# Sums of squares of q by products with a column of ones, and fewer transpositions of constants

## The chip, the core and the metric

The program runs on one core of a Trainium2 chip, in one launch. The metric is the device time in microseconds (us) of one execution. Three executions of the kernel before were timed: 1227.67, 1227.69 and 1228.21 us, median 1227.69 us. A fourth was profiled: 1226.6 us from its first to its last instruction.

The engines in the profile: PE (TensorE, the matrix engine; PEld are its loads of the stationary operand), DVE (VectorE), ACT (ScalarE), POOL (GpSimd) and SP (which here only issues transfers).

## What is computed

Two decoder layers with a residual stream of 512 positions by 1024 channels. The first has gated linear attention as its mixer, the second a gated DeltaNet; each is followed by a gated feed-forward network with a causal convolution of width 3, and each of the four sublayers ends in a layer norm. What concerns us is the second mixer, cut to its core:

```python
proj = x @ w_in
qkv, gate, beta_lin, a_lin = split(proj)
qkv = silu(causal_dwconv(qkv, conv_w))          # width 4
q, k, v = split(qkv)                            # 8 heads of 128 channels
qc = l2_normalize(q_by_head) * 128 ** -0.5      # x * rsqrt(sum(x*x) + 1e-6), per position and head
kc = l2_normalize(k_by_head)
m = tril(k_beta @ k.T * decay, -1)              # per head and chunk of positions
sol = triangular_solve(I + m, [v * beta, k_beta * exp(bcum)])
qk = q @ k.T * decay
# per chunk: v_new = u - w @ S ; o = q_dec @ S + qk @ v_new ; S = S * decay + k_dec.T @ v_new
y = (rms_norm(o, norm_w) * silu(gate)) @ w_out
```

The sum of squares of q, for each of 512 positions and 8 heads, is needed only at the very end: the kernel leaves q unscaled and folds 1/|q| into the scale of the output rows.

## The kernel before

All products are float32 or float32 split in two halves (`wh`, `wl` and `xh`, `xl`: three products stand for one). Activations lie with channels on the 128 partitions and positions along the row, except where a product needs it the other way round; then a 128x128 block is transposed on PE by a product with the identity (`tr`, line L226 of the profile, and `tr4` for four of them). All other products go through `mm` (L208).

The program is written as one main stream of large products (tiles `fm`, `tm`, `fold`) with small tasks between them. Tasks are Python generators; a planner's clock, `self.clk`, is moved on by an estimate for each product (0.11 us for a transposition, 0.00175 us per column for a float32 product), and after every few large products `pump` runs the tasks that are due. A task yields the time that it wants to wait. So the position of small work in the stream is set by these estimates. In the first stage the order on PE is fixed as written; from the second half of the first mixer on a scheduler may still move instructions of different tasks against each other. Each engine then runs its own list strictly in order.

The second mixer (`gdn`) first projects k (8 heads), then v, then q, one head for each `fm` bank of 24 large products. `gdn_conv` (L1541 to L1545) turns a bank into a head: one ACT operation, three on DVE, then SiLU on ACT. For each pair of q heads `q_done` starts `q_task` 6 planner microseconds later. `q_task` first calls `squares`: it transposes the four 128x128 blocks of each head into a PSUM bank `qT` (L226), so that positions lie on partitions, and eight ACT operations square a block each and sum its rows into `ssq` (L1625). Then it forms k-by-q products `pq` (L208) and DVE multiplies them into the decay matrix (L1682). `norms(0)` (L1818) turns `ssq` into 1/|q| once all eight heads are there.

Meanwhile `base` inverts 32x32 triangles for all heads and chunks at once, 31 pairs of DVE operations (L1703, L1705) spread over the projections. Its result `tt` is copied to `m` (L1708), both go to DRAM (`dinvt`, L1710; `dinv`, L1709), and come back laid out for PE, four pairs of heads one after another, in small transfers on the queues of SP and POOL: `T` (L1722) and `rm` (L1725). `inverses` then builds the 128x128 inverses from them in ten steps of small products with results `V` and `R`, each step at least 3.2 planner microseconds after the one before. Step 0 makes `V` of pair 0; step 1 makes `V` of pair 1 and, from the copied `V` of pair 0 (L1769 on ACT, L1770 on DVE), `R` of pair 0.

Rows of constants (layer norm weights, convolution taps) are loaded with channels along the row and transposed once by `columns`: one transposition and one copy for each set of rows, for the first mixer (sets of 4 and 2 rows) and, at planner time 64, for everything else (sets of 32, 32, 88, 44, 88, 44, 96 and 1 rows).

Of the kernel before, what the change touches and what calls it, by code (L numbers as in the profile page):

```python
# [12 lines left out]
AF = mybir.ActivationFunctionType  # L13
ALU = mybir.AluOpType

P = 128
# [51 lines left out]
def blk(i, n=P):  # L68
    return slice(i * n, i * n + n)


class Trunk:
# [646 lines left out]

    def columns(self, specs):  # L720

        loads = []
        for i, (rows, n, dst) in enumerate(specs):
            if i % 4 == 0:
                t = self.slot("rows")
            r = t[:, blk(i % 4)]
            self.nc.gpsimd.dma_start(r[:n, :], rows)
            loads.append((r, n, dst))
        yield 4.0 + len(specs)
        ps, at = self.psum("cols"), 0  # L730
        for r, n, dst in loads:
            self.tr(ps[:, at:at + n], r[:n, :], n)
            at += n
        at = 0
        for _, n, dst in loads:
            self.nc.vector.tensor_copy(dst, ps[:, at:at + n])
            at += n


    def x_part(self, tb, hf):  # L740

# [806 lines left out]
    def gdn(self, li, g, b):  # L1548
        nc = self.nc
# [9 lines left out]
        ssq, rr = self.own([P, 2, DH, 4], "gd_ssq"), self.own([P, DH, 4], "gd_rr")  # L1559
        bt = self.own([P, 4, 64], "gd_bt")  # L1560
        q, k, v, am, rm, pj = ([None] * DH for _ in range(6))
# [56 lines left out]

        def squares(hd):

            for i in (hd, hd + 1):
                pt = self.psum("qT")
                self.tr4(pt, q[i])
                for ck in range(4):
                    nc.scalar.activation(pt[:, blk(ck)], pt[:, blk(ck)], AF.Square, accum_out=ssq[:, 0, i, ck:ck + 1])  # L1625
                self.set(("ssq", 0, i))

        def k_done(ps, hd):
# [4 lines left out]
        def q_done(ps, hd):  # L1633
            q[hd] = self.gdn_conv(ps, hd, self.slot("conv"))
            if hd % 2:
                self.spawn(q_task(hd - 1), CONV_DELAY)
# [36 lines left out]
                self.set(("am", i), 2.0)  # L1673

        def q_task(hd):
            squares(hd)
            for i in (hd, hd + 1):
                yield from self.until(("am", i))
            for i in (hd, hd + 1):
                pq = self.psum("pq")  # L1680
                self.mm4(pq, k[i], q[i])
                nc.vector.tensor_mul(pj[i], pj[i], pq)  # L1682
                self.set(("pj", i), 1.2)
# [343 lines left out]
```

## Time and profile before

| | |
|---|---|
| median of three timed executions | 1227.69 us |
| profiled execution, first to last instruction | 1226.6 us |
| PE busy | 1219.4 us, 99% |
| PEld busy | 1029.4 us, 84% |
| DVE busy | 928.2 us, 76% |
| ACT busy | 604.0 us, 49% |
| granted TensorE clock | 1.000 |
| chain that ended last, share of PE | 98% |
| PE busy in 692 to 746 us, where the q heads' tasks stand | 53.99 of 54.00 us |
| DVE, ACT busy in the same stretch | 43.35, 29.93 us |

The page gives the profiled execution's span alone; the time measured around an execution is larger by what lies before its first and after its last instruction. "Busy" of PE counts modelled ends of pipelined products, so two of them overlap in the rows; the distance between starts tells what one costs in the stream. A group row ends in the summed busy time, the mean duration in ns, and the idle time of the engine just before.

### The profile page before, as it was taken

How to read it: one execution, taken by the hardware profiler on the slowest of the kernel's cores; microseconds unless marked ns; L12 is line 12 of the kernel's file. 1: busy time of each engine (PE TensorE's matmuls, PEld its weight loads, DVE VectorE, ACT ScalarE, POOL GpSimd, SP SyncE). 2: the span in 40 equal slices, each digit the busy share in tenths (PEclk: the TensorE clock that was granted, in tenths of full speed). 3: DMA queues.
4: the chain of work that ended last, by engine and by line, in shares of the span. 5: the costliest groups of instructions: out<-in, count | busy, mean ns of one | idle time of the engine just before them, and what ended most of it. 6: DMA issues, size and time to landing. Idle time of an engine off the chain costs nothing.

```text
span 1226.6 us, 17147 instructions
## 1 busy us (share of the span) xinstructions
PE 1219.4 (99%) x6530; PEld 1029.4 (84%) x6530; DVE 928.2 (76%) x1539; ACT 604.0 (49%) x1066; POOL 115.1 (9%) x159
## 2 busy tenths in 40 slices
PE   9999999999999999999999999999999999999998
PEld 8888888988888888888888888988988888888886
DVE  4966996688957895667779975688687966796667
ACT  5654764544434443554678555644644434443440
POOL 4000000700000000001152030200520000000000
PEclk9999999999999999999999999999999999999999
DMA  7432253542443123333344351245442263223321
GB/s 205 117 107 69 87 179 102 167 120 69 136 139 102 53 68 114 111 105 104 104 129 129 99 139 37 77 130 155 123 135 69 82 192 87 89 82 103 106 66 69
DMA packets 171186, 133.67 MB, mean 109 GB/s; under 512 B 16390, under 2 KB 140362, under 8 KB 171104
## 3 DMA queue, kind: packets, MB, share of 16 engines
q1 hardware_dynamic: 166272, 123.62, 34.2%
q0 software_dynamic: 3872, 8.30, 2.1%
q8 instruction: 51, 0.84, 0.3%
q10 hardware_dynamic: 960, 0.66, 0.2%
q14 instruction: 31, 0.25, 0.1%
HBM read 126.77 MB, written 5.78 MB: 108 GB/s over the span
## 4 chain that ended last, share of the span: by engine, by line
PE 98%; DMA 1%; SPq 0%; DVE 0%; ACT 0%; issue 0%; DVEq 0%
PE fm L208 54%; PE tm L208 20%; PE fold L208 16%; PE o L208 2%; PE xT L226 1%; DMA raw<-in_gla_w_in_dram 1%; PE pq L208 1%; PE pg L208 1%; PE vn L208 1%; PE yT L226 1%; PE V L208 0%; PE qs L208 0%; PE s L208 0%; PE ks L208 0%; PE ds L208 0%; PE sa L208 0%
## 5 line engine op out<-in xcount | busy, mean ns | idle before, releaser
L208 PE MATMUL fm<-xh,wh 128*128 128x512 f32 (+2 forms) x1096 | 400.4, 368 | 0.7 <-ACT xh L698 0.7
L208 PE MATMUL fm<-xl,wh 128*128 128x512 f32 (+2 forms) x1096 | 398.5, 366 | 0.0
L208 PE MATMUL fm<-xh,wl 128*128 128x512 f32 (+1 forms) x1072 | 391.5, 367 | 0.4 <-DVE wl L698 0.4
L698 DVE TENSOR_TENSOR wl<-raw,wh 128x1024 fp32r<-128x1024 f32 (+1 forms) x162 | 200.6, 1241 | 160.5 <-ACT wh L698 160.3
L698 ACT CAST wh<-raw 128x1024 fp32r<-128x1024 f32 (+1 forms) x163 | 168.9, 1038 | 221.6 <-PE fm L208 145.1
L208 PEld LDWEIGHTS fm<-xh,wh 128*128 128x128 f32 (+1 forms) x1096 | 205.4, 188 | 34.1 <-ACT xh L698 0.9
L208 PEld LDWEIGHTS fm<-xl,wh 128*128 128x128 f32 (+1 forms) x1096 | 205.4, 188 | 33.0
L208 PEld LDWEIGHTS fm<-xh,wl 128*128 128x128 f32 x1072 | 201.2, 189 | 33.8 <-DVE wl L698 0.6
L993 DVE SCALAR_TENSOR_TENSOR conv<-fm,ffn_cw,conv 128x511 f32<-128x511 f32 x112 | 83.5, 746 | 9.4 <-ACT conv L991 8.0
L208 PE MATMUL fold<-wh,fh 128*128 128x512 f32 x224 | 87.6, 391 | 0.0
L208 PE MATMUL fold<-wh,fl 128*128 128x512 f32 x224 | 87.2, 389 | 0.0
L208 PE MATMUL fold<-wl,fh 128*128 128x512 f32 x224 | 87.2, 389 | 0.0
L698 ACT CAST wh<-b 128x1024 fp32r<-128x1024 f32 x48 | 49.8, 1053 | 74.6 <-PE fold L208 31.1
L1011 ACT ACTIVATE conv<-conv 128x512 f32<-128x512 f32 x44 | 27.8, 632 | 69.0 <-DVE conv L993 69.0
L698 DVE TENSOR_TENSOR wl<-b,wh 128x1024 fp32r<-128x1024 f32 x48 | 58.0, 1223 | 4.7 <-ACT wh L698 4.7
L1543 DVE SCALAR_TENSOR_TENSOR conv<-fm,gdn_cw,conv 128x511 f32<-128x511 f32 (+2 forms) x72 | 54.1, 790 | 5.1 <-ACT conv L1541 4.5
L208 PE MATMUL tm<-wh,xh 128*128 128x512 f32 x128 | 52.6, 411 | 0.0
L208 PEld LDWEIGHTS fold<-wh,fh 128*128 128x128 f32 x224 | 42.0, 188 | 9.8 <-DVE h L1082 1.2
L208 PE MATMUL tm<-wl,xh 128*128 128x512 f32 x128 | 50.1, 391 | 0.0
L208 PE MATMUL tm<-wh,xl 128*128 128x512 f32 x128 | 50.0, 391 | 0.0
L208 PEld LDWEIGHTS fold<-wh,fl 128*128 128x128 f32 x224 | 42.0, 188 | 8.8
L208 PEld LDWEIGHTS fold<-wl,fh 128*128 128x128 f32 x224 | 42.1, 188 | 8.6
(359 smaller groups left out, 1932.5 us busy)
## 6 DMA issues: line engine op xcount, KB each, us to landing
raw<-in_ffn_w_in_dram SPq DMA_DIRECT2D x88, 512.0 KB, 3.9
raw<-in_gdn_w_in_dram SPq DMA_DIRECT2D x32, 512.0 KB, 4.1
raw<-in_ffn_w_out_dram SPq DMA_DIRECT2D x28, 512.0 KB, 3.7
raw<-in_gla_w_in_dram SPq DMA_DIRECT2D x26, 512.0 KB, 3.7
b<-in_ffn_w_out_dram SPq DMA_DIRECT2D x24, 512.0 KB, 5.5
raw<-in_gla_w_out_dram SPq DMA_DIRECT2D x8, 512.0 KB, 3.8
raw<-in_gdn_w_out_dram SPq DMA_DIRECT2D x8, 512.0 KB, 3.8
h<-in_x_dram SPq DMA_DIRECT2D x8, 256.0 KB, 4.7
```

Source lines behind the costliest of these rows:

```text
L208: t = self.nc.tensor.matmul(out, a, b, start=start, stop=stop, skip_group_check=joined)
L226: t = self.nc.tensor.transpose(out, a, self.ident[:n, :n])
L698: return self.nc.scalar.copy(dst_h, src), self.nc.vector.tensor_sub(dst_l, src, dst_h)
L993: nc.vector.scalar_tensor_tensor(a[:, d:], ps[:, :S - d], tap(2 - d), a[:, d:], ALU.mult, ALU.add)
L1011: nc.scalar.activation(a, a, AF.Gelu)
L1543: self.conv = nc.vector.scalar_tensor_tensor(a[:, d:], ps[:, :S - d], tap(3 - d), a[:, d:], ALU.mult, ALU.add)
```

## The change

`squares` no longer transposes. ACT squares a whole head into a new tile `sq`, the task yields 3 planner microseconds, and then PE multiplies each of the four blocks of each head, as the stationary operand, with a column of ones: a 128-row result of one column, which is the sum over channels for 128 positions. Eight such columns of two heads stand in one PSUM bank `qq` and DVE copies them into `ssq`. The planner's clock is moved by 0.062 us for each of these products. `columns` packs the sets of rows into tiles of up to 128 rows, so that (128, 121, 88, 88) rows take four transpositions where eight stood, and the six rows of the first mixer one where two stood; the copies out are as many as before.

```diff
     def columns(self, specs):
-        loads = []
-        for i, (rows, n, dst) in enumerate(specs):
-            if i % 4 == 0:
-                t = self.slot("rows")
-            r = t[:, blk(i % 4)]
-            self.nc.gpsimd.dma_start(r[:n, :], rows)
-            loads.append((r, n, dst))
+        tiles, loads = [], []
+        for rows, n, dst in sorted(specs, key=lambda t: -t[1]):
+            at = next((i for i, used in enumerate(tiles) if used + n <= P), None)
+            if at is None:
+                at = len(tiles)
+                tiles.append(0)
+            loads.append((rows, n, dst, at, tiles[at]))
+            tiles[at] += n
+        t = self.slot("rows")
+        for rows, n, dst, i, r in loads:
+            self.nc.gpsimd.dma_start(t[r:r + n, blk(i)], rows)
         yield 4.0 + len(specs)
-        ps, at = self.psum("cols"), 0
-        for r, n, dst in loads:
-            self.tr(ps[:, at:at + n], r[:n, :], n)
-            at += n
...
+        ps = self.psum("cols")
+        for i, n in enumerate(tiles):
+            self.tr(ps[:, i * P:i * P + n], t[:n, blk(i)], n)
+        for _, n, dst, i, r in loads:
+            self.nc.vector.tensor_copy(dst, ps[:, i * P + r:i * P + r + n])
...
         def squares(hd):
+            sqs = []
             for i in (hd, hd + 1):
-                pt = self.psum("qT")
-                self.tr4(pt, q[i])
-                for ck in range(4):
-                    nc.scalar.activation(pt[:, blk(ck)], pt[:, blk(ck)], AF.Square, accum_out=ssq[:, 0, i, ck:ck + 1])
+                sqs.append(self.slot("sq"))
+                nc.scalar.activation(sqs[-1], q[i], AF.Square)
+            yield 3.0
+            pt = self.psum("qq")
+            for n in range(8):
+                self.mm(pt[:, n:n + 1], sqs[n // 4][:, blk(n % 4)], self.one)
+                self.clk += 0.06
+            nc.vector.tensor_copy(ssq[:, 0, hd:hd + 2, :].rearrange("p h c -> p (h c)"), pt[:, :8])
+            for i in (hd, hd + 1):
                 self.set(("ssq", 0, i))
...
         def q_task(hd):
-            squares(hd)
+            yield from squares(hd)
```

The change moves instructions in the second mixer. PE's list at the first pair of q heads, before (rows are in the engine's order, `x4` is four in a row, numbers behind names tell buffers apart):

```order
L226 MATMUL vT_6138<-ident_86,conv_5895 128x128 x4
L226 MATMUL vT_6147<-ident_86,conv_5962 128x128 x4
L226 MATMUL qT_6156<-ident_86,conv_6007 128x128 x4
L226 MATMUL qT_6165<-ident_86,conv_6074 128x128 x4
L208 MATMUL pq_6174<-conv_6007,conv_5045 128x128 x4
L208 MATMUL pq_6180<-conv_6074,conv_5075 128x128 x4
L208 MATMUL fm_6131<-xh,wh_6015 128x512
```

And PE's list at the same pair with the change:

```order
L208 MATMUL fm_6125<-xl,wh_6009 128x512
L208 MATMUL fm_6125<-xh,wl_6010 128x512
L208 MATMUL qq_6198<-one_87,sq_6150 128x1 x4
L208 MATMUL qq_6198<-one_87,sq_6152 128x1 x4
L208 MATMUL pq_6208<-conv_6001,conv_5039 128x128 x4
L208 MATMUL pq_6214<-conv_6068,conv_5069 128x128 x4
L208 MATMUL fm_6232<-xh,wh_6076 128x512
```

The block of small products of a pair stands 18 large products later than before, at the end of the bank and no longer in its first quarter.

PE's list from the end of step 0 of the inverses to the start of step 1, before:

```order
L208 MATMUL V_6424<-T_6213,am_5156 32x32
L226 MATMUL qT_6443<-ident_86,conv_6284 128x128 x4
L226 MATMUL qT_6452<-ident_86,conv_6368 128x128 x4
L208 MATMUL pq_6461<-conv_6284,conv_5256 128x128 x4
L208 MATMUL pq_6467<-conv_6368,conv_5295 128x128 x4
L208 MATMUL fm_6485<-xh,wh_6292 128x512
L208 MATMUL fm_6485<-xl,wh_6292 128x512
L208 MATMUL fm_6485<-xh,wl_6293 128x512
L208 MATMUL fm_6485<-xh,wh_6292 128x512
L208 MATMUL fm_6485<-xl,wh_6292 128x512
L208 MATMUL fm_6485<-xh,wl_6293 128x512
L208 MATMUL V_6493<-T_6267,am_5243 32x32
```

And PE's list there with the change (`V_6397`, `V_6398` are step 0, `V_6430`, `R_6432` are step 1, `V_6396` is the copied `V` of step 0):

```order
L208 MATMUL fm_6366<-xl,wh_6228 128x512
L208 MATMUL V_6397<-T_6181,am_5141 32x32 x4
L208 MATMUL V_6397<-T_6181,am_5150 32x32 x4
L208 MATMUL fm_6366<-xh,wl_6229 128x512
L208 MATMUL V_6398<-T_6181,am_5141 32x32 x4
L208 MATMUL V_6398<-T_6181,am_5150 32x32 x4
L208 MATMUL V_6430<-T_6245,am_5237 32x32
L208 MATMUL R_6432<-rm_6183,V_6396 32x32
L208 MATMUL R_6432<-V_6396,rm_6183 32x32
```

Step 1 follows step 0 at once; before, the third pair's block and six large products stood between them. The third pair's block now stands behind step 2.

SP's list of transfers from the end of `base` on, before:

```order
L1709 DMA dinv<-m_818_4908 128x1024
L1710 DMA dinvt<-tt_4907 128x1024
L1725 DMA rm_6215<-dinv 32x4x32
L1725 DMA rm_6217<-dinv 32x4x32
L1725 DMA rm_6215<-dinv 32x4x32
L1725 DMA rm_6217<-dinv 32x4x32
L1722 DMA T_6213<-dinvt 32x8x32 x3
```

And SP's list with the change (`T_6181` and `rm_6183` are pair 0, `T_6245` is pair 1; lines are shifted by six):

```order
L1716 DMA dinvt<-tt_4901 128x1024
L1715 DMA dinv<-m_817_4902 128x1024
L321 DMA raw_6942<-in_gdn_w_in_dram 128x2x512
L1728 DMA T_6181<-dinvt 32x8x32
L1731 DMA rm_6183<-dinv 32x4x32
L1731 DMA rm_6185<-dinv 32x4x32
L1728 DMA T_6181<-dinvt 32x8x32 x2
L1731 DMA rm_6183<-dinv 32x4x32
L1731 DMA rm_6185<-dinv 32x4x32
L1728 DMA T_6245<-dinvt 32x8x32
```

The first pair's `T` stands earlier among its transfers, and a load of weights (`raw_6942`) that was behind all `T` and `rm` is now ahead of them. On DVE all three convolution operations of the fourth q head and one copy of `qq` now stand ahead of the last operations of `base` or right behind them; before, the three stood behind its last.

More of the change, by code (lines that the diff above doesn't have):

```diff
@@ L720, in columns @@
     def columns(self, specs):
-        loads = []
-        for i, (rows, n, dst) in enumerate(specs):
-            if i % 4 == 0:
-                t = self.slot("rows")
-            r = t[:, blk(i % 4)]
-            self.nc.gpsimd.dma_start(r[:n, :], rows)
-            loads.append((r, n, dst))
-        yield 4.0 + len(specs)
-        ps, at = self.psum("cols"), 0
-        for r, n, dst in loads:
-            self.tr(ps[:, at:at + n], r[:n, :], n)
-            at += n
[L734 to L737, printed above, removed]
+        tiles, loads = [], []
[9 more added lines that the diff above has]
+            self.nc.gpsimd.dma_start(t[r:r + n, blk(i)], rows)
+        yield 4.0 + len(specs)
+        ps = self.psum("cols")
[3 more added lines that the diff above has]
+            self.nc.vector.tensor_copy(dst, ps[:, i * P + r:i * P + r + n])
     def x_part(self, tb, hf):
```

## The prediction

> **What bounds the kernel now.** I read the page's first and fourth parts, then the stretch of the second mixer in which the q heads' tasks stand, by stretches and in order of time. From the page and the stretch:
>
> ```profile
> span 1226.6 us, 17147 instructions
> PE 1219.4 (99%) x6530; PEld 1029.4 (84%) x6530; DVE 928.2 (76%) x1539; ACT 604.0 (49%) x1066; POOL 115.1 (9%) x159
> PE 98%; DMA 1%; SPq 0%; DVE 0%; ACT 0%; issue 0%; DVEq 0%
> 692.00:746.00 54.00, 53.99 (x649) 44.95 (x648) 43.35 (x99) 29.93 (x102) 9.83 (x19) 1.00 0.36 97
> ```
>
> PE is the chain: 98% of it, and in the 54 us that the change touches it has 0.01 us without a product (the second number is PE's; the granted clock is 1.00). So whatever PE issues more or less there moves the end by as much, and ACT's work, 29.93 of 54 us, counts only where PE waits for it. The question is what one small product costs in PE's stream. Starts in order of time:
>
> ```profile
> 692.23 1.04 PE L226 MATMUL qT<-ident,conv 128*128 128x128 f32 x8
> 693.11 1.95 PE L208 MATMUL pq<-conv,conv 128*128 128x128 f32 x16
> 694.81 0.48 PE L208 MATMUL fm<-xh,wh 128*128 128x512 f32 x1
> 695.13 0.40 PE L208 MATMUL fm<-xl,wh 128*128 128x512 f32 x1
> 695.36 0.39 PE L208 MATMUL fm<-xh,wl 128*128 128x512 f32 x1
> 705.79 1.03 PE L226 MATMUL qT<-ident,conv 128*128 128x128 f32 x8
> 706.66 1.95 PE L208 MATMUL pq<-conv,conv 128*128 128x128 f32 x16
> 718.87 1.09 PE L226 MATMUL qT<-ident,conv 128*128 128x128 f32 x8
> 719.80 1.95 PE L208 MATMUL pq<-conv,conv 128*128 128x128 f32 x16
> ```
>
> Eight transpositions hold the stream for 693.11 - 692.23 = 0.88 us, 0.11 us each. Eight float32 products `pq` stand as 16 passes and hold it for 694.81 - 693.11 = 1.70 us, again 0.11 us a pass: a transposition is one pass, a float32 product two. A large product takes 695.36 - 695.13 = 0.23 us. The change replaces 32 transpositions by 32 float32 products, so 32 passes by 64, each with one column moving and not 128.
>
> **The transpositions removed.** The three pairs above take 0.88, 0.87 and 0.93 us. The fourth:
>
> ```profile
> 735.76 0.66 PE L226 MATMUL qT<-ident,conv 128*128 128x128 f32 x4
> 736.17 0.48 PE L208 MATMUL tm<-wh,xh 128*128 128x512 f32 x1
> 736.66 0.42 PEld L226 LDWEIGHTS qT<-ident,conv 128*128 128x128 f32 x4 [0.32 <-ACT conv L1545]
> 737.15 1.95 PE L208 MATMUL pq<-conv,conv 128*128 128x128 f32 x16
> ```
>
> 0.41 and 0.49 us, and between them a `tm` product that lasts 0.49 us to the next start where 0.23 is usual: 0.26 us of waiting for the SiLU of the last head. Removed: 0.88 + 0.87 + 0.93 + 0.41 + 0.49 + 0.26 = **3.84 us**. The wait goes because the products come 3 planner microseconds later, behind large products.
>
> **The products added.** What sets a pass with one column? Its 128-column stationary operand must still be loaded. The loads, by shape (mean ns after the comma):
>
> ```profile
> L208 PEld LDWEIGHTS V<-T,am 32*32 32x32 f32 x128 | 3.2, 106 | 1.5 <-issue 0.7 <-DVE dt L1682 0.4 <-ACT T L1772 0.4
> L208 PEld LDWEIGHTS sa<-e,e 128*64 128x64 f32 x64 | 3.6, 136 | 0.7 <-ACT na L1334 0.4 <-issue 0.4
> L208 PEld LDWEIGHTS fm<-xh,wh 128*96 128x96 f32 x16 | 2.6, 161 | 0.0
> L208 PEld LDWEIGHTS pq<-conv,conv 128*128 128x128 f32 x64 | 7.5, 192 | 0.0
> L226 PEld LDWEIGHTS qT<-ident,conv 128*128 128x128 f32 x32 | 3.5, 140 | 0.6 <-ACT conv L1545 0.3
> ```
>
> From 32 to 128 columns a load grows by 192 - 106 = 86 ns, 0.9 ns a column, so the part that grows is about 0.115 us at 128 columns; the rest, some 77 ns, all loads share, and they overlap in it, or `pq` could not run at 0.11 us a pass. The load goes on beside the product before it. For `pq` load and product are about equal, and either could set the 0.11 us; with one column moving, the product shrinks and the load does not. One place in the trace has few columns on a full-width load, the last warm-up pass of 64 columns and the first transposition behind it:
>
> ```profile
> L772 PE MATMUL warm<-one x6: 221/901/1222, 1.0 to 4.3; 128*128 128x512 f32 x4, 128*128 128x64 f32 x2
> 4.29 0.19 PEld L772 LDWEIGHTS warm<-one 128*128 128x128 f32 x1 [0.24 <-issue]
> 4.35 0.37 PEld L226 LDWEIGHTS xT<-ident,h 128*128 128x128 f32 x3
> 4.45 0.39 PE L226 MATMUL xT<-ident,h 128*128 128x128 f32 x2
> ```
>
> The load for the 64-column pass begins at 4.29, the next load at 4.35, and the product behind that only at 4.45, 0.16 us after the first of the two loads began, though 64 columns are half of what `pq` moves in 0.11 us. Loads, not products, paced it.
>
> So I take 0.11 us a pass: 64 x 0.11 = **7.04 us**. The bounds: an unhidden load at 0.192 us would make 12.3 us; if loads did not count, the nearest row is the 32-column `V` below, 32 passes from 718.10 to 718.87, 0.024 us each, 1.5 us. `pq` is the nearer row by shape, type and place, hence its price.
>
> [...]
>
> The ACT work shrinks: 32 squares with a read of the sum become eight squares of 512. PE waits for these squares at the first product of each head; 18 large products stand between, 4.1 us at 0.23 us. Were they gone, a square of about 0.63 us (as the SiLU of the same shape) would be exposed for each head. The four copies of `qq` lie on DVE beside PE's work. The later `ssq` of the last pair is wanted only after the recurrence. All this I cost at nothing. The SiLU's row:
>
> ```profile
> L1545 ACT ACTIVATE conv<-conv 128x512 f32<-128x512 f32 x7 | 4.4, 632 | 12.6 <-DVE conv L1543 12.6
> ```
>
> **The constants.** Eight transpositions of constants, and what follows:
>
> ```profile
> 83.97 1.51 PE L226 MATMUL cols<-ident,rows 32*128 32x32 f32 x8
> 85.41 0.50 PE L208 MATMUL tm<-wh,xh 128*128 128x512 f32 x1
> ```
>
> 1.44 us for eight, 0.18 each; the four that remain have more columns and wait for up to three transfers each, so I give them 0.25: 1.0 us. With one saved in the first mixer, **-0.5 us** (bounds 0 and -0.9).
>
> **The inverses.** Step 1 now follows step 0 at once, and reads its copied `V`:
>
> ```profile
> 718.10 0.84 PE L208 MATMUL V<-T,am 32*32 32x32 f32 x32
> 718.99 0.43 DVE L1770 COPY V<-V 32x256 f32<-32x256 f32 x1 [1.91 <-PE V L208]
> 723.07 0.21 PE L208 MATMUL V<-T,am 32*32 32x32 f32 x1
> ```
>
> The copy ended at 719.42, 0.55 us after PE had gone on at 718.87; 3.65 us of other products covered that. The cover is gone: PE waits about 0.6 us, and step 0, cut in two halves, overlaps less in the array, 0.2 us. **+0.8 us** (bounds 0 and, with a late transfer, 3.6; below). Step 1 also needs `T` of pair 1. Its transfers:
>
> ```profile
> 708.16 0.18 DVE L1705 TENSOR_TENSOR tt<-tt,tmp 128x31 f32<-128x31 f32 x1
> 708.26 0.74 DVE L1543 SCALAR_TENSOR_TENSOR conv<-fm,gdn_cw,conv 128x511 f32<-128x511 f32 x1
> 710.45 0.42 SPq L1710 DMA_DIRECT2D dinvt<-tt  x1
> 715.11 1.86 SPq L1722 DMA_DIRECT2D T<-dinvt  x4
> dinvt<-tt SPq DMA_DIRECT2D x1, 512.0 KB, 4.0
> T<-dinvt SPq DMA_DIRECT2D x12, 32.0 KB, 2.1
> raw<-in_gdn_w_in_dram SPq DMA_DIRECT2D x5, 512.0 KB, 3.7
> ```
>
> `base` ended at 708.34. With three convolutions (about 0.66 us each from start to start) and a copy ahead of it, it ends near 710.5; `dinvt` leaves at 710.6 and lands at 714.6; the last `T` of pair 1 is the twelfth issue from there, 11 x 0.46 = 5.1 us later, and lands 2.1 us after that, at 721.8. PE starts step 0 at 718.10 + 1.76 (32 passes of 0.11 for 16 in the first two pairs) - 0.23 = 719.6, is through at 720.6, waits to 721.2, and reaches the half of step 1 that wants that `T` about 721.7. So nothing more is lost, but nothing is to spare either; before, step 1 began at 723.07. Queued behind a late `T` on PE is the main stream itself.
>
> **The sum.** -3.84 + 7.04 - 0.5 + 0.8 = +3.5 us on a profiled span of 1226.6, so 1230.1; the median timed before, 1227.69, lies 1.1 us above that span, so the forecast is **1231.2 us**.
>
> **The rivals.** *The load of weights holds up `T`.* `raw_6942` now stands on SP ahead of all `T` and `rm`. It moves 512 KB in 3.7 us and may push them back by 2 to 3.6 us; PE then waits at step 1 by as much: 1233.2 to 1234.8, say 1234. For it: the two queue in one list. Against: before, two transfers of 512 KB one behind the other landed 3.2 and 4.0 us after issue, so they share.
>
> *Loads are hidden and the transfers pin step 1.* At 0.024 us a pass the products cost 1.5 us, 5.5 less. But PE then reaches step 1 some 2.7 us earlier, and waits for the `T` that lands at 721.8: -3.84 + 1.5 - 0.5 + 0.2 + 2.9 = +0.3, 1228.0. For it: the `V` row. Against: those are 32 columns wide.
>
> *Loads are hidden and nothing waits*, the other side: -3.84 + 1.5 - 0.5 + 0.2 = -2.6, 1225.1. The place is the 64 passes of `qq`; with my other terms break-even is at (3.84 + 0.5 - 0.8) / 64 = 0.055 us a pass. It needs both a load half as long as its slope and a `T` earlier than worked out.
>
> [...]
>
> **How the numbers follow.** Forecast 0.58, late `T` 0.18, pinned 0.16, faster 0.08. The forecast's own range is 1229.6 to 1232.8: a pass of 0.10 to 0.125 us gives -0.6 to +1.0, the constants 0.4 either way, the wait -0.8 to +0.4. The whole range, 1227.3 to 1234.6, leaves out the fast rival and the late transfer's far end. A change of 0.2%, 2.5 us, is about what a measurement of this kernel can tell from none. Slower by more: most of the forecast's cases (0.49) and the late transfer, 0.67. Within: the pinned case and the forecast's low end, 0.25. Faster: 0.08.
>
> **What would show it.** `qq` would stand as 64 passes in PE's rows, eight products of a pair 1.7 to 1.9 us from the first start to that of `pq`; 0.4 us would prove the load hidden. `R` of step 1 should wait about 0.6 us for the copies of `V`; a wait for a transfer there means the first or second rival. The constants should take about 1.0 us. I am wrong if a pass of `qq` costs under 0.055 us, or if PE shows a wait elsewhere, such as for the squares on ACT.

## The result and the profile after

| | before | with the change |
|---|---|---|
| median, beside each other on one chip | 1227.93 us (1227.67 to 1228.21) | 1235.15 us (1233.12 to 1238.52) |
| ratio, 95% interval | | 1.0062 [1.0049, 1.0074] |
| profiled execution, time and span | span 1226.6 us | 1233.26 us, span 1231.5 us |
| mean granted clock of the executions | 1.000 | 0.998, 0.998, 0.996, 0.994 |

The kernel is slower, as forecast, but by more: 4 us above the forecast of 1231.2 and 0.6 above the range. And it no longer repeats: its executions lie 5.4 us apart, those of before 0.5, and the longer ones have the lower mean clock. The profiled one is near the lower end. Of all executions below, three ran much longer than the others of their kernel (one of before at 1348 us, one with a padded tile at 6122, one of the last kernel at 1518), and no reading rests on them.

The page, and the stretch of the q heads (its length in us, busy time of PE, PEld, DVE, ACT, POOL, granted clock, DMA share, GB/s):

```profile
span 1231.5 us, 17168 instructions
PE 1224.9 (99%) x6557; PEld 1035.1 (84%) x6557; DVE 928.8 (75%) x1543; ACT 599.3 (49%) x1010; POOL 114.8 (9%) x159
PE 99%; DVE 0%; ACT 0%; issue 0%; DVEq 0%; POOL 0%; POOLq 0%
692.00:746.00 54.00, 53.65 (x632) 44.73 (x632) 36.67 (x79) 21.87 (x38) 9.17 (x17) 0.97 0.35 97
```

PE is the chain as before. Two things are new in the last row: PE has 0.35 us without a product, and the granted clock is 0.97 where it was 1.00. Starts in order of time, at the constants, the first pair of q heads and the inverses:

```profile
84.41 0.53 PE L226 MATMUL cols<-ident,rows 128*128 128x128 f32 x4
84.73 0.48 PE L208 MATMUL tm<-wh,xh 128*128 128x512 f32 x1
...
694.36 1.84 PE L208 MATMUL qq<-one,sq 128*128 128x1 f32 x16
696.07 2.03 PE L208 MATMUL pq<-conv,conv 128*128 128x128 f32 x16
697.86 0.48 PE L208 MATMUL fm<-xh,wh 128*128 128x512 f32 x1
...
717.76 0.69 PE L208 MATMUL V<-T,am 32*32 32x32 f32 x16
718.37 0.49 PE L208 MATMUL fm<-xh,wl 128*128 128x512 f32 x1
718.80 0.69 PE L208 MATMUL V<-T,am 32*32 32x32 f32 x18
719.39 0.18 PE L208 MATMUL R<-rm,V 32*32 32x32 f32 x1
...
720.34 0.22 PE L208 MATMUL V<-T,am 32*32 32x32 f32 x2 [0.20 <-DMA T<-dinvt]
720.70 0.21 PE L208 MATMUL R<-rm,V 32*32 32x32 f32 x1
```

The eight products of `qq` hold the stream for 696.07 - 694.36 = 1.71 us, 0.11 us a pass: the main term came true. The constants take 0.32 us, not 1.0. Steps 0 and 1 of the inverses run into one another, with two short stalls (from start to start 0.4 us before 720.34 and 0.3 before 720.70). What follows stands in no step of the prediction. The clock in this trace changes only after whole multiples of 3.413 us (5.04 to 721.84 us at 1.00, to 725.25 at 0.50, to 1230.43 at 1.00: 210, 1 and 148 of them), so here are windows of that length, counted back from the point at which it changes:

```profile
715.01:718.43 3.42, 3.42 (x30) 2.64 (x28) 0.53 (x1) 1.20 (x2) 3.42 (x8) 1.00 0.61 105
718.43:721.84 3.41, 3.06 (x100) 2.55 (x100) 2.56 (x5) 2.10 (x5) 3.15 (x6) 1.00 0.46 78
721.84:725.25 3.41, 3.41 (x55) 2.33 (x54) 0.49 (x2) 0.00 (x0) 0.00 (x0) 0.50 0.29 45
725.25:728.67 3.42, 3.42 (x49) 2.79 (x48) 0.97 (x4) 0.36 (x1) 0.00 (x0) 1.00 0.23 36
```

After the window that holds the two steps, the clock is 0.50 for one window and then 1.00 again; in it a large product takes 0.427 us from start to start where 0.227 is usual.

To see where the time went I added up, over the same 300-odd large products of the second mixer (some 690 to 815 us), the distance from each product's start to the next start, by the tile that it makes. Sums over the trace's rows, us:

| tile | before | after | what it is |
|---|---|---|---|
| large products | 74.18 | 75.06 | `fm`, `tm` |
| `qT` / `qq` | 3.58 | 6.99 | the change |
| `pq` | 6.82 | 7.40 | same products |
| `V` | 3.27 | 4.26 | same products |
| `R` | 6.30 | 7.40 | same products |
| all else | 34.79 | 34.72 | the recurrence and transpositions |
| sum | 128.94 | 135.83 | +6.89 |

Half of the loss in this stretch, 3.41 us, is the new products against the transpositions. The other half is in products that the change does not touch. (The span grew by 4.9 us only: the stretch begins 2.0 us earlier than before, mostly by the constants.) Two causes were then to be told apart: a changed order of the steps, and the clock.

### The profile page after: what moved, and what is told of

It is laid out like the page before. It is cut to its first block, busy times and chain, and to the rows that moved or that the text cites. A ratio compares the mean times of both kernels' runs of the same rounds, so it can differ in the third digit from the quotient of the medians.

```text
span 1231.5 us, 17168 instructions
## 1 busy us (share of the span) xinstructions
PE 1224.9 (99%) x6557; PEld 1035.1 (84%) x6557; DVE 928.8 (75%) x1543; ACT 599.3 (49%) x1010; POOL 114.8 (9%) x159
## 4 chain that ended last, share of the span: by engine, by line
PE 99%; DVE 0%; ACT 0%; issue 0%; DVEq 0%; POOL 0%; POOLq 0%
PE fm L208 54%; PE tm L208 20%; PE fold L208 16%; PE o L208 2%; PE xT L226 1%; PE pq L208 1%; PE pg L208 1%; PE vn L208 1%; PE qq L208 1%; PE yT L226 1%; PE V L208 0%; PE qs L208 0%; PE s L208 0%; PE ks L208 0%; PE ds L208 0%; PE warm L772 0%
## 5 line engine op out<-in xcount | busy, mean ns | idle before, releaser
L993 DVE SCALAR_TENSOR_TENSOR conv<-fm,ffn_cw,conv 128x511 f32<-128x511 f32 x112 | 83.4, 745 | 10.2 <-ACT conv L991 8.8
```

The lines of the kernel that those rows point to most:

```text
L993: nc.vector.scalar_tensor_tensor(a[:, d:], ps[:, :S - d], tap(2 - d), a[:, d:], ALU.mult, ALU.add)
```

## The experiments

The time of before beside which each was timed is 1227.87 to 1227.96 us. "The stream" below is the sum just described.

**The constants alone**: before, with the first part of the change's diff (`columns`) and nothing else.

> The kernel before with the new packing of the constants' rows and nothing else. Theory, from the shift between the large products of the two traces: -0.16 us at the first mixer's rows and -1.2 us behind the eight sets, so 1227.9 - 1.4 = 1226.5 us, and the large product behind the four transpositions starts 0.3 to 0.6 us after the first of them where it stood 1.44 us behind. Rival, the prediction's term: -0.5 us, 1227.4 us. Either way the granted clock stays at 1.00 up to the tail, since nothing of the second mixer moves.

Measured: 1226.73 us against 1227.87, ratio 0.9992 [0.9983, 1.0001]. The difference of medians is -1.1 us, between the two theories and nearer the first; the interval takes in no change at all, so the timing alone does not settle a microsecond. The trace's 0.32 us for the four transpositions, where I had set 1.0, does.

**What sets the price of a pass.** The first 32 of each block's 128 columns as the stationary operand, in the changed kernel with the delay of the inverses at 24 (the next but one below). It leaves out the sums of the other 96 positions of a block; DVE copies the 32 rows four times, which the diff below leaves out.

```diff
-                self.mm(pt[:, n:n + 1], sqs[n // 4][:, blk(n % 4)], self.one)
+                self.mm(pt[:32, n:n + 1], sqs[n // 4][:, blk(n % 4)][:, :32], self.one)
```

> The changed kernel with the delay of 24, each product taking only the first 32 of the 128 columns of a block as its stationary operand (so q's norms are left wrong: 96 of 128 positions get those of others). Theory, the load sets the pace of a pass: near the 0.024 us of the 32-column passes of V, up to 0.05, so 64 x 0.06 to 0.088 = 3.8 to 5.6 us less than the delay of 24 alone: 1225.1 to 1226.9 us. Rival, a float32 pass with one moving column has a floor of 0.11 us whatever its load: 1230.7 us, no change.

Measured: 1226.22 us against 1230.72 with full blocks. By shape (ns: least, median, most) and by start:

```profile
L208 PEld LDWEIGHTS qq<-one,sq x64: 106/113/113, 694.6 to 738.7; 128*32 128x32 f32 x64
694.61 0.67 PE L208 MATMUL qq<-one,sq 128*32 128x1 f32 x16
695.21 2.05 PE L208 MATMUL pq<-conv,conv 128*128 128x128 f32 x16
```

Sixteen passes in 0.60 us, most of them 0.032 us apart where full blocks stand 0.112 apart. The load's width sets the price; the rival's floor of 0.11 us falls. A load's own row is longer than the distance between passes: 113 ns at 32 columns, 192 at 128.

**More moving columns.** The column of ones read 64 times, so that a pass moves 64 columns and its load is the same.

```diff
-                self.mm(pt[:, n:n + 1], sqs[n // 4][:, blk(n % 4)], self.one)
-                self.clk += 0.06
+                self.mm(pt[:, blk(n, 64)], sqs[n // 4][:, blk(n % 4)], self.one.to_broadcast([P, 64]))
+                self.clk -= 0.05
```

> The changed kernel, with the column of ones read 64 times (64 moving columns instead of one; the first of each 64 result columns is used). Loads of the stationary operand set the pace (theory): a pass still takes 0.11 us and the block of eight products still 1.8 us. Rival, the number of moving columns counts: less than 0.11 us was possible with one, or more is needed with 64. The clock: if it is dropped by windows in which the array has little to do, the blocks of qq now count as work and only steps 0 and 1 of the inverses, still nearly back to back, can drop it: at most one stretch of 3.4 us at 0.5, executions between 1231 and 1233 us, none at 1237 or 1238. If only waits of PE drop it, as many stretches as with the change and executions spread from 1233 to 1238.5 us again.

Measured: 1231.79 us, six executions from 1231.71 to 1231.93, no half-clock stretch in the profiled one before the end of the program. A pass stays at 0.112 us (`qq` 7.18 us in the stream). But in this build two large products stand between steps 0 and 1, so it shows what is left without half clock, not which of its two edits did it. Hence the next two.

**Step 1 apart from step 0.** The changed kernel with one number different, which brings PE's list around steps 0 and 1 back to that of before, with `qq` for `qT` (the fourth pair's block is cut by `tm` products instead); then both edits together.

```diff
-INV_DELAY = 18.0
+INV_DELAY = 24.0
```

> The changed kernel with the delay of the inverses at 24 planner us, not 18: PE's list is again that of before there (step 0, the block of the third pair, six large products, step 1), with qq for qT. Theory: the products cost +3.3 us net of the transpositions, the constants -1.4, and step 1 waits for nothing, so 1227.9 + 1.9 = 1229.8 us as long as the clock stays at 1.00. If waits at steps 0 and 1 alone dropped the clock, no stretch at 0.5 is left and all executions lie within 0.6 us. If little work in the array drops it, step 0 with the qq block beside it (2.6 us with hardly a moving column) drops it in some executions: 1229.8 in some, 1.7 us more for each window in others. Rival, the later inverses hold up the recurrence: a wait at its products and more than 1231 us at a clock of 1.00.

> Both edits: 64 moving columns and the delay of 24. Theory (little work in the array drops the clock): no window is left that is as empty as that of the drop, so no stretch at 0.5, and all executions at 1229.8 us within 0.6 us. Rival, waits drop it: the same as with the delay of 24 alone. Rival, 64 columns cost more than one: above the fastest of the delay of 24 alone by 64 times the difference of a pass.

Measured: with one column 1230.72 us, six executions at 1230.4 to 1230.7 and three at 1231.8 to 1232.0 with a clock of 0.999; with 64 columns 1230.15 us, all eleven from 1230.04 to 1230.48. As the theory of little work has it, the three long ones vanish where the passes move more, at the same price per pass. The three were not profiled, and three of nine against none of eleven is thin; the dose below settles it. The order of the steps by itself costs 1231.79 - 1230.15 = 1.6 us (64 columns in both; in the stream `V` and `R` account for 1.13).

**The change again**, for more executions.

> The changed kernel itself once more, for more executions. Theory: a window of 3.41 us at half clock costs up to 1.7 us, and where the windows fall differs from execution to execution, so the times stand in groups about 1.7 us apart above the one without a window, 1231.4 us, with the lower mean clock at the longer times: 0.999, 0.998, 0.996, 0.994. Rival, another disturbance lengthens the long executions: spread without steps and without relation to the clock.

Measured: 1233.11, 1234.00, 1234.01, 1236.69 and 1237.09 us, clocks 0.998, 0.999, 0.999, 0.996, 0.996. (The 1231.4 in the expectation is the span, not the time, of an execution with a clock of 0.998, the same as that of the profiled one with one window.) There are groups, but the middle one does not fit steps of 1.7 us and has the higher clock at the longer time, so something else differs too; what, no trace shows. The profiled execution, the longest of these, lost three windows (columns as above):

```profile
726.39:729.80 3.41, 3.41 (x57) 3.37 (x58) 1.18 (x3) 0.63 (x1) 0.00 (x0) 1.00 0.23 36
729.80:733.21 3.41, 3.41 (x24) 3.19 (x24) 1.38 (x4) 1.05 (x2) 0.00 (x0) 0.50 0.62 163
733.21:736.63 3.42, 3.42 (x11) 2.62 (x11) 1.97 (x3) 0.58 (x1) 0.00 (x0) 0.50 0.00 0
746.87:750.28 3.41, 3.41 (x51) 2.99 (x51) 1.97 (x3) 0.75 (x2) 0.00 (x0) 1.00 0.24 40
750.28:753.69 3.41, 3.41 (x17) 3.41 (x18) 1.13 (x4) 0.00 (x0) 0.00 (x0) 0.50 0.31 114
```

Its stream sums to 139.37 us against 135.83 with one window: 1.8 us for each of the two more. In the windows ahead of these PE is busy for all of the 3.41 us. The first, at 726.39, holds the `qq` products of the third pair, the one at 746.87 those of the fourth.

**The dose.** Each product of the ones done twice, with one moving column and with 64, both at the delay of 24.

```diff
+            for n in range(8):
+                self.mm(pt[:, 8 + n:9 + n], sqs[n // 4][:, blk(n % 4)], self.one)
+                self.clk -= 0.00175
```

> The changed kernel with the delay of 24, and each product of the ones done twice (the second into columns that nobody reads): 128 passes more than that, or rather 64, one moving column each. Loads pace them (theory): +64 x 0.112 = +7.1 us, so 1230.7 + 7.1 = 1237.8 us at a clock of 1.00. If little work in the array drops the clock (theory), the 3.6 us of each pair with one moving column per pass leave a window nearly empty in most executions: stretches of 3.4 us at 0.5 at two or more of the four blocks, 1239 to 1246 us, spread over several us. If only waits of PE drop it: no stretch, 1237.8 us within 0.6, since PE waits for nothing inside a block.

```diff
+            for n in range(8):
+                self.mm(p2[:, blk(n, 64)], sqs[n // 4][:, blk(n % 4)], self.one.to_broadcast([P, 64]))
+                self.clk -= 0.112
```

> The same doubling with 64 moving columns for each product. Theory: the price of a pass is that of its load, so again +7.1 us, 1230.15 + 7.1 = 1237.3 us, and with 64 columns in each pass no window is nearly empty: no stretch at 0.5 before the tail, executions within 0.6 us. Rival, the clock follows the length of the block and not its work: the same stretches and times as with one column.

Measured: 1248.58 us with one column, 1238.30 with 64. Two windows around the first pair, of the narrow kernel and of the wide one:

```profile
696.05:699.46 3.41, 3.41 (x32) 3.41 (x32) 0.83 (x4) 0.68 (x2) 0.53 (x1) 1.00 0.02 5
699.46:702.87 3.41, 3.41 (x14) 3.02 (x14) 3.41 (x7) 0.00 (x0) 0.00 (x0) 0.50 0.30 78
...
696.06:699.47 3.41, 3.41 (x32) 3.41 (x32) 3.20 (x9) 0.94 (x2) 0.00 (x0) 1.00 0.02 5
699.47:702.88 3.41, 3.41 (x21) 2.96 (x20) 3.31 (x7) 0.64 (x1) 0.00 (x0) 1.00 0.00 0
```

The narrow one has 20.5 us at half clock in all (three single windows and three in a row), so about 10.2 us lost; the two times differ by 10.3. The wide kernel has none before its tail, the end of the program where PE runs out of products. The first windows of both stand at the same place, with 32 passes, as many loads and PE busy throughout by its rows; of PE's work only the moving columns differ. So here the clock followed what the products moved, one column (0.50 in the next window) or 64 (1.00), not gaps in PE's rows. The wide one took 1.0 us more than expected, 0.7 of it in `R` (7.04 us in the stream, 6.30 without doubling); the narrow one lay 2.6 us beyond its expected end, because it lost six windows in all, three of them in a row.

**Steps close together, without `qq`.** Before, with the delay at 16.

```diff
-INV_DELAY = 18.0
+INV_DELAY = 16.0
```

> The kernel before with the delay of the inverses at 16 planner us, not 18: step 0 is cut in two halves and only one large product stands between it and step 1, as with the change, but the third pair's transpositions and pq follow, and no qq is there. Theory: the order of the steps costs what it cost between the two kernels with 64 columns and delays of 18 and 24, 1231.79 - 1230.15 = 1.6 us, here with waits at the transfers of T up to 2.5: 1229 to 1230.4 us; the clock stays at 1.00, since transpositions and pq fill the window. Rival, steps standing close drop the clock by themselves: a stretch of 3.4 us at 0.5 there, 1.7 us more, and times that spread in steps.

Measured: 1230.12 us, ten executions from 1229.33 to 1231.75. The median is where it was expected; the clause that the clock stays is wrong for the profiled execution, the longest of the ten (windows, columns as above):

```profile
719.14:722.55 3.41, 3.41 (x102) 3.01 (x102) 2.10 (x3) 2.83 (x5) 3.41 (x8) 1.00 0.41 68
722.55:725.96 3.41, 3.41 (x18) 3.41 (x17) 3.31 (x9) 2.57 (x15) 0.79 (x2) 0.50 0.37 58
```

So the rival holds here: the steps packed together lower the clock without any `qq`, and with PE busy for the whole window. One reading covers both. Count, for each window, the moving columns of the products that start in it, each weighted by the size of its stationary operand as a share of 128x128, the largest here (a 32x32 product counts a sixteenth). Fifteen large products, a full window at 0.227 us each, make 7,680. Over all traces of this case, from 9 us after the start to the tail, windows at full clock with up to 1,224 were followed by half clock in seven of seven cases (the change 1,216; this kernel 1,216; the doubled one 31, 156, 1,173; the change again 1,168 and 1,224). Between 1,488 and 2,048 it went both ways (1,488 and 1,984 not, 1,776 and 2,048 so), and above 2,048 it never happened in some 6,600 windows. Before, the emptiest window had 2,944. In the tails, where PE does stand idle, 256 and 512 were followed by half clock in four of four traces, 1,024 in two of three, and 1,536 and more in none: the edge is not sharp. Without the weights the order is lost: 4,096 moving columns were followed by half clock (the change, this kernel) and 1,984 were not (the doubled one with 64). The weighting is mine and fits these data; a rule of the chip is not shown by them.

**One pass in place of two.** The squares and the ones as float32r, for which the trace has 32 passes of `qq` where it has 64 with float32, at 64 columns and the delay of 24; then three kernels for what came out.

```diff
+        self.oner = self.keep([P, 1], "oner", F32R)
+        nc.vector.tensor_copy(self.oner, self.one)
...
-                sqs.append(self.slot("sq"))
+                sqs.append(self.slot("sq", F32R))
...
-self.one.to_broadcast([P, 64])
+self.oner.to_broadcast([P, 64])
```

> The kernel with 64 columns and the delay of 24, with the squares and the ones written as float32r, so that each product is one pass and not two. Theory, the number of full-width loads is the price: 32 passes of 0.112 us fewer, 1230.15 - 3.6 = 1226.6 us, level with the kernel before with the new constants alone (1226.73 us). Rival, a float32r pass with few moving columns takes 0.22 us: 1230.2 us, no change. No stretch at 0.5.

Measured: 1232.27 us, though `qq` fell from 7.12 to 3.42 us in the stream as expected. The loss is elsewhere: large products of other stages, `fold` above all, stood 0.229 to 0.232 us apart instead of 0.227. The new tile moves what is allocated behind it by 4 bytes on each partition (one of 32 columns moves it by 128, which the first expectation below overlooks). So: a tile of 32 columns; the float32 kernel with such a tile unused; and a tile of 128 columns.

```diff
-        self.oner = self.keep([P, 1], "oner", F32R)
+        oner = self.keep([P, 32], "oner", F32R)
...
+        self.oner = oner[:, :1]
```

> The one-pass kernel with its column of ones in a tile of 32 columns (128 bytes a partition) and not of one (4 bytes), so that the tiles allocated behind it lie where they lay in the other kernels. In the one-pass kernel the qq passes came to 3.42 us where 7.12 stood, as expected, but large products in some twelve stretches of all stages ran at 0.229 to 0.232 us in place of 0.227 and took the gain back. Theory, the shift by 4 bytes slows them: with the shift gone 1226.6 us. Rival, the copy of the ones or the float32r products themselves do it: 1232.3 us again.

```diff
+        oner = self.keep([P, 32], "oner", F32R)
+        nc.vector.tensor_copy(oner, ones)
```

> The kernel with 64 columns and the delay of 24, plus one unused float32r tile of 32 columns behind the identity (and a copy of the ones into it), so that what is allocated later lies 128 bytes further on each partition; the products of the ones stay float32. If the place of the tiles slows the stretches of large products, this kernel shows the same steps of 0.2 us as the padded one-pass kernel: some +3 us less what is given back, 1233 to 1234 us. If the float32r products do it: 1230.15 us, no change.

```diff
-        oner = self.keep([P, 32], "oner", F32R)
+        oner = self.keep([P, 128], "oner", F32R)
```

> The one-pass kernel with its column of ones in a tile of 128 columns, 512 bytes a partition, as much as the two new tiles take in the kernel with the squares moving, where no such steps appear. If the place decides and 512 bytes are harmless: 1226.6 us and no steps. If the float32r products decide: 1230.8 us and the steps again.

Measured: 1230.81 us (128 bytes, float32r), 1234.59 (128 bytes, unused, float32), 1226.72 (512 bytes, float32r). The theory of the 4 bytes alone fell with the first; the second and third settle it: the place of the tiles does it, whatever the products. Groups by form, of the float32 kernel without and with the unused tile:

```profile
L208 PE MATMUL fold<-wh,fl 128*128 128x512 f32 x224 | 87.2, 389 | 0.0
```

```profile
L210 PE MATMUL fold<-wh,fl 128*128 128x512 f32 x224 | 88.4, 395 | 0.0
```

6 ns a product over all of this group, and 4.4 us more in the whole kernel (1234.59 against 1230.15). Why 128 bytes hurt and 512 do not, no run here shows.

**The operands change places.** The squares (float32r) move, 512 columns at once, and eight columns of `pick`, ones in the head's own and zeros elsewhere, are stationary. DVE gathers the pairs' 8x512 results, and four transpositions turn them at the end. New constants, delay 24.

```diff
+            for n in range(2):
+                self.mm(pt[:DH, :], self.pick[:, blk(hd + n, DH)], sqs[n], start=n == 0, stop=n == 1)
+            if hd:
+                nc.vector.tensor_add(sqt, sqt, pt[:DH, :])
+            else:
+                nc.vector.tensor_copy(sqt, pt[:DH, :])
...
+            for j in range(4):
+                self.tr(ps[:, blk(j, DH)], sqt[:, blk(j)], DH)
```

> The version that ought to beat both: the operands change places. A head's squares (float32r) are the 512 moving columns, and 8 columns with ones in the head's own one are the stationary operand, so a head takes one large product with a load of 8 columns; DVE adds the pairs' 8x512 results into one tile, and four transpositions of 8 rows turn it at the end. Delay 24, new constants. Theory: from the kernel before with the new constants, 1226.73 us, -3.84 for the transpositions and the wait, + 8 x 0.227 + 4 x 0.11 = +2.26, and up to +0.4 where small products begin and end: 1225.1 to 1225.6 us, no stretch at 0.5. Rival, PE waits for the squares or for DVE at these products: 1226.7 us, no gain.

Measured: 1226.52 us, 0.9 us over the top of the expected range. That is near the rival's time, but not for its reason: `qq` and `qT` came to 1.94 + 0.34 = 2.28 us, as worked out. Instead `V` came to 3.94 and `R` to 6.57, 0.8 more than in the kernel with the new constants alone. Two changes of delay followed, the first 23 for the inverses, the second 20 with no wait between squares and products:

```diff
-INV_DELAY = 24.0
+INV_DELAY = 23.0
```

> The kernel with the squares moving, with the delay of the inverses at 23: six large products now stand between step 0 and the third pair's block. In the run at 24, qq and its four transpositions cost 2.28 us as expected, but V and R cost 10.51 us in the stream where the kernel before has 9.57. If the direct neighbour of step 0 did that, V and R return to about 9.6 and the time to 1225.6 us; if the later split (a half of step 4 and a half of R around one large product), which is still there, the time stays at 1226.5 us.

```diff
-INV_DELAY = 24.0
+INV_DELAY = 20.0
...
-            yield 3.0
+            yield 0.0
```

> The same with the delay at 20 and no wait between the squares and their products: the half step behind the last pair is not split any more, but step 2 is (24 and 16 products around two large ones). If the split behind the last pair cost the 0.9 us, 1225.6 us; if any split costs as much, 1226.5 us again. PE may wait for the first square, up to 0.6 us a pair: then up to 1228 us.

Measured: 1226.37 us, `V` unchanged at 3.94, so the neighbour of step 0 was not it; and 1232.29 us, a miss on every count: PE stood 3.0 us waiting for `T`, and two windows at half clock followed. The window ahead of the two, with 2.3 us of that idle time in it, is the 2,048 above. What was left to blame was a cut step (starts in order of time, in the first kernel with the squares moving):

```profile
739.59 1.14 PE L213 MATMUL V<-T,am 64*64 64x64 f32 x16
740.66 0.50 PE L213 MATMUL tm<-wh,xl 128*128 128x512 f32 x1
741.09 1.14 PE L213 MATMUL R<-rm,V 64*64 64x64 f32 x16
742.16 0.50 PE L213 MATMUL tm<-wh,xh 128*128 128x512 f32 x1
```

`V` and `R` of one step stand apart, and each takes 1.07 us. The last kernel keeps the steps whole:

```diff
-CONV_DELAY = 6.0
+CONV_DELAY = 5.0
-INV_DELAY = 24.0
+INV_DELAY = 23.0
```

> The kernel with the squares moving, with delays of 5 (not 6) from the last q head to its task and 23 for the inverses: no step of the inverses is cut by a large product any more. In the runs at 24 and 23, V came to 3.94 us where the kernel with whole steps had 3.16, in the one place where half of V of step 6 stands before one large product. If the cut costs that, V returns to 3.2 to 3.4 and the time to 1225.6 to 1225.9 us; if not, 1226.4 us. No stretch at 0.5.

Measured: 1224.97 us against 1227.93, ratio 0.9976 [0.9966, 0.9986], nine of ten executions within 0.75 us and no half clock before the tail. `V` is 3.20 us, as expected, and `R` 6.26. The time is 0.6 us below the expected range: `V` and `R` account for 1.05 us of the 1.55 gained on the first of these kernels, and the rest is not taken apart. Of the 3.0 us gained on before, 1.1 are the constants. The same step, whole, by starts:

```profile
738.86 0.27 PE L213 MATMUL V<-T,am 64*64 64x64 f32 x1
738.86 0.27 PE L213 MATMUL R<-rm,V 64*64 64x64 f32 x1
...
739.78 0.22 PE L213 MATMUL R<-rm,V 64*64 64x64 f32 x1
739.93 0.50 PE L213 MATMUL tm<-wl,xh 128*128 128x512 f32 x1
```

Alternating, `V` and `R` start within 0.01 us of each other and the pair takes 1.07 us together, what each took alone.

## Why the prediction was right or wrong

| step of the prediction | forecast, us | measured, us | from |
|---|---|---|---|
| transpositions removed | -3.84 | -3.58; that the wait of 0.26 is gone is not shown apart | stream of before |
| 64 passes of `qq` | +7.04 | +6.99 | stream after |
| constants | -0.5 (0 to -0.9) | about -1.1 | constants alone; 0.32 for 1.44 |
| `pq` behind `qq` | no term | +0.4 with steps apart (+0.6 in the profiled change) | stream |
| order of the inverses | +0.8 (0 to 3.6) | +1.6 at full clock | delays 18 and 24 at 64 columns |
| granted clock, and the stalls | taken as 1.00 | +1.9 in the stream of the profiled execution; others took up to 6.7 more | after against 64 columns at the same delay, whose order differs by two large products |

**The main term was right, for the reason given.** A pass with one moving column costs its load: 0.11 us at 128 columns, the same with 1 and with 64 moving columns, and 0.032 at 32. The two rivals with hidden loads fall. The third, a late `T` behind the load of weights, appears only as the wait of 0.2 us at 720.34.

**The constants were sized too small.** I gave each of the four transpositions 0.25 us for transfers that had landed; they cost 0.08.

**The inverses were half right.** Step 1 does stall behind step 0, by 0.3 to 0.4 us in two places. But the greater part of the price is in cut steps, for which 0.2 us was allowed. The two halves of step 0 take 718.37 - 717.76 = 0.61 and 719.39 - 718.80 = 0.59 us (the second with two products of step 1) where the whole took 0.77. The two kernels with 64 columns show it at full clock: step 0 takes 0.62 us whole and 2 x 0.62 cut, step 2 takes 1.07 whole and 2 x 0.63 cut, together 0.8 us; step 1 takes 0.88 us where it stands apart and 1.21 behind step 0, 0.3 us. A later step, in the last experiments, lost the overlap of `V` and `R` where a large product cut it. For the change itself, whose order is closer still, the shares are argued from these rows, not measured apart. That the wait for `T` stayed small is partly luck: `dinvt` left SP at 708.48 us and PE came to step 0 at 717.76, both some 2 us earlier than worked out (710.6 and 719.6).

**The step that failed is the one that had no term**: the clock. The prediction quoted 1.00 for the stretch of before and went on as if that were a property of the stretch. With nearly the same order and no empty window, the kernel with 64 columns takes 1231.79 us, 0.6 above the forecast and inside its own range; the change's executions lie 1.3 to 6.7 us above that. The profiled one with one window lies 1.5 us above, the one with three 5.3, which is 1.5 to 1.8 us for each. That the sum at full clock comes so near the forecast is partly luck: the constants gave 0.6 us more than forecast, the order cost 0.8 more and `pq` 0.4. And whether a median lies above 1234.6 is chance too: the first four executions have 1235.15 us, the five later ones 1234.01. The missing term is the same in both. Both of the change's effects leave little moving in a window (1,216 weighted columns in the one before the drop): passes that move one column, and steps of 32x32 products packed together. Where a window of 3.41 us falls on them differs from one execution to the next (by 1.1 us between the two traces of the change, counted from their first instruction), which would make the times spread.

Ahead of the tail the half clock came in whole windows: 3.41 us in the profiled change, 3.41 and 6.83 in the change again, 20.5 in all in the doubled kernel. A PE without products was not needed for it: in the doubled kernel PE was busy for 3.41 of 3.41 us, as the profile counts it with modelled ends, and the next window stood at 0.50.

## What to carry to other kernels

A pass here cost 0.112 us with a stationary operand of 128 columns, whether 1 or 64 columns moved, and 0.032 with one of 32, so put the wide operand on the moving side. The same sums took 6.99 us with the squares stationary in float32, 3.42 in float32r, and 2.28 with the squares moving in float32r: the larger part of that gain is the pass saved, the rest is the exchange. Before moving small products together, count the columns that move in each 3.41 us around them; a PE that is busy by its rows (3.41 of 3.41 us) did not keep the clock. And look at what an edit does to neighbours that it does not name: here a delay changed by a few planner microseconds or a tile of 128 bytes moved the time by 1.6 to 5.8 us.

## What was not expected of the hardware

- Half clock with a busy PE: ahead of the tail, up to 1,224 weighted columns of 7,680 in 3.41 us were followed by it in seven of seven windows, above 2,048 in none, between them in some.
- Two kinds of small products that alternate overlap: 32 passes of 64x64 took 1.07 us, and 16 of one kind alone 1.07 us as well.
- A tile of 128 bytes, unused, made large products of `fold` 389 to 395 ns long and the kernel 4.4 us slower; 512 bytes did not. The cause is open.
